# The second attention of a two-layer backbone: 18 filling steps set first, the others spread evenly and tied to the scores, bias tables requested at a group's middle, maxima two tiles later, eight raw weight buffers

## The chip, the core and the metric

The kernel runs on one core of a Trainium2 chip. Five engines work there side by side and meet at semaphores: PE (matrix products), DVE (vector), ACT (activation), POOL (a second, general vector engine) and SP, which here only issues transfers. Each engine takes its instructions in the order in which the built program lists them. An instruction that waits holds up everything behind it on the same engine. Transfers are issued by SP (a few by ACT) and carried out by 16 DMA engines that all queues share.

The metric is the device time of one launch in microseconds (us), the median of several runs. Beside it stands one profiled execution with its own time; all waits and durations below are from that one.

## What is computed

Two layers work on 1024 latent tokens and 256 context tokens of width 1024. Layer 0 is two kinds of grouped attention; layer 1, the odd one, joins a convolution branch (C) with a two-dimensional neighbourhood attention (D). The change is in layer 1, and there in D and in the product that follows it:

```python
cv, cgl, cg, dq, dk, dv, dg = split_cols(h_lat @ w_in, ODD_WIDTHS)
oc = conformer_conv(cv, cgl, cg, dw_w, dw_b, ln_g, ln_b)
def d_row(args):                       # one row of the 16x64 grid, all 8 heads
    r, qr = args
    rs = jnp.clip(r - kh // 2, 0, rows - kh)
    kr = lax.dynamic_slice_in_dim(k_grid, rs, kh, axis=1)   # 8 rows of keys
    ...
    bias = rpb[:, dr_idx][:, :, dc_idx] + col_mask[None, None]
    kk = jnp.concatenate([c_dk, kr], axis=1)                # 256 context keys first
    vv = jnp.concatenate([c_dv, vr], axis=1)
    return gqa_attend(qr, kk, vv, bias).reshape(bsz, GRID_W, D_W)   # softmax attention
od = lax.map(d_row, (jnp.arange(rows), q_rows))
y_lat = jnp.concatenate([oc, od * jax.nn.silu(dg)], axis=-1) @ w_out
x_lat = x_lat + g_l[:, None, :] * y_lat
return rms_norm(x_lat, final_g)
```

Everything is f32. The kernel splits each factor of a large product into a high and a low part and adds three matmuls, so that each such product counts three times.

## The kernel before, in words

**Groups and tiles.** The attention of layer 1 is cut into 16 groups: 8 heads (`hd`) times two column halves of the grid (`hf`). A group has 512 queries and seven score tiles: the context keys 0 to 127 (512 queries wide), five tiles of 128 grid keys (256, 352, 512, 320 and 224 queries wide) and the context keys 128 to 255 (512). A score tile `st` is two matmuls, L465 (`KAt` with `QH`) and L469 (`KBt` with `QL`). For the five grid tiles DVE adds the bias table `bs` (L474) and ACT takes the exponential (L475); for the context tiles ACT does it alone (L477). ACT casts the result to the high part `ph` (L296), POOL or DVE forms the low part `pl` (L299), and three matmuls L409 to L411 add it into the group's `ov`. There are two `st` banks. Each score tile's `ov` products are written in the code three tiles after it (`LOOK1`).

**Maxima.** Before a group's first score, its row maxima must be known. `maxes` makes six `mx` tiles on PE (L1342, L1350) from `QH` and the group's keys `KAt`; DVE reduces them (L1344, and L1351 together with the mask table `bm`); a transposition `trn` and L388 put them into `QL`. This preparation is done two groups ahead: at the start of group g the code asks for the queries of group g+2 (L1301 to L1303) and starts the maxima `LEAD` tiles later, four here.

**What a group's start requests.** `start` asks SP for the next group's bias table `bs` (832 KB, two buffers), at every other group for the next head's keys `KAt` (L361, two transfers of 384 KB, two buffers), and for this group's values `Vt`. Keys and queries go into buffers that the last score tile of the group before still reads, so they can be issued only after it. ACT copies the new keys' upper half into `KBt` (L555). In the group's middle `gate` asks for the gate values `gt` (L1320).

**Filling work.** The attention's own chain is long, so other matmuls are woven in: `d_proj(2)` and `d_proj(3)` (projections `p1` of the last four heads; 31 steps each of up to three dk, nine matmuls), `out1_part` (the output product `po1`: 32 steps with six matmuls, then 8), and `ends` (30 steps). `weave` runs `WV[i]` steps of the attention, two to a tile, and spreads a part's filling steps among them. The weights of a filling part come by `load_w` in pieces of 128 rows: SP loads a raw piece `wr` (L329, three buffers), ACT casts it to `wh` (L296), and POOL or DVE forms `wl` (L299).

**What sets the order.** The code is traced in program order; each instruction gets a priority from its place, and `later(FL[1])`, with -98, moves filling steps ahead. A list scheduler then simulates time and fixes each engine's queue: it takes, by priority, what its model of the chip holds to be ready, so an instruction written later can stand earlier. `issue_after` adds only an order between two instructions of one engine. With a lag of 0 for the first two parts, 6 and 12 for the others, a filling step is held behind the score that many tiles back, or not held at all.

The lines that the steps below touch are `d_proj` and `proj1` (L318 to L320 by way of `mm3`), `attn_gen`, `weave`, `gate`, `start`, `load_w`, and the calls at the end.

## Time and profile before

| | us |
|---|---|
| median of 3 runs (1557.06 to 1565.91) | 1563.07 |
| the profiled execution's own time | 1555.72 |
| its span, first to last instruction | 1553.9 |
| PE busy | 1449.1 |
| DVE, ACT, POOL busy | 1123.3, 759.8, 833.5 |

The profiled execution is 7.35 us shorter than the median and lies below all three runs but within half a percent of the median. A page of the profile gives busy times, which for PE are upper bounds since matmuls overlap; the windows view cuts the span into stretches and gives each engine's busy time, the granted PE clock (1.00 is full) and the share of the 16 DMA engines that was busy. The view of waits adds up, for each pair of line and releaser, how long the engine sat idle. In the names, `st<-QH,KAt` is written from right to left: `st` is made of `QH` and `KAt`. The second attention begins at 1212.7 us with the first maxima; its last score tile ends at 1516.9 us, and the program ends at 1553.9 us.

### The profile page before, as it was taken

What the parts mean: (1) busy time and instruction counts of PE and PEld (TensorE: products, weight loads), DVE (VectorE), ACT (ScalarE), POOL (GpSimd) and SP (SyncE); (2) the same over time, 40 slices, a digit from 0 to 9 for tenths busy, and PEclk for the clock granted to TensorE, in tenths of its full rate; (3) what the DMA queues carried; (4) which work ended last, traced back from release to release, by engine and by line L of the source; (5) the groups of instructions that cost most, each with busy time, mean ns of one, the idle gap of its engine ahead of it and who ended that gap; (6) DMA issues with size and microseconds to landing.
All of it is one profiled execution on the core that took longest, in us unless ns stands there. A gap on an engine that the chain in (4) does not pass through costs nothing.

```text
span 1553.9 us, 22052 instructions
## 1 busy us (share of the span) xinstructions
PE 1449.1 (93%) x6984; PEld 1172.3 (75%) x6984; DVE 1123.3 (72%) x2172; ACT 759.8 (49%) x1545; POOL 833.5 (54%) x762
## 2 busy tenths in 40 slices
PE   6989989999999989899999889999999999799995
PEld 1878868887789678678887668888787787687784
DVE  4998898689858666654577677999755457586776
ACT  2721354445454755565455555443434455545563
POOL 1561464555555676675455666664542443545574
PEclk9999999999999999999999999999999999899996
DMA  9548245423441124631111121213456888788623
GB/s 339 194 146 270 79 125 174 147 64 121 151 129 44 54 89 143 207 115 56 42 45 35 68 95 57 80 63 123 158 178 222 272 225 263 221 264 240 192 92 109
DMA packets 185614, 221.01 MB, mean 142 GB/s; under 512 B 17421, under 2 KB 139481, under 8 KB 185497
## 3 DMA queue, kind: packets, MB, share of 16 engines
q1 hardware_dynamic: 178832, 208.03, 43.1%
q10 hardware_dynamic: 6664, 11.57, 2.3%
q8 instruction: 55, 0.90, 0.2%
q14 instruction: 63, 0.51, 0.1%
HBM read 159.51 MB, written 60.03 MB: 141 GB/s over the span
## 4 chain that ended last, share of the span: by engine, by line
PE 67%; DVE 12%; DMA 11%; issue 3%; POOL 3%; ACT 2%; SPq 2%; DVEq 0%; ACTq 0%; POOLq 0%
PE p L320 6%; PE p L318 6%; PE p L319 6%; PE ov L409 4%; PE ov L410 4%; PE ov L411 4%; PE st L465 4%; PE po L318 4%; PE st L469 4%; PE po L319 4%; PE po L320 4%; PE pq L320 2%; PE pq L319 2%; PE pq L318 2%; DMA mw<-in_mod_w_dram 2%
## 5 line engine op out<-in xcount | busy, mean ns | idle before, releaser
L299 POOL TENSOR_TENSOR pl<-pf,ph 128x512 fp32r<-128x512 f32 (+4 forms) x321 | 399.9, 1258 | 270.7 <-ACT ph L296 218.9
L299 POOL TENSOR_TENSOR wl<-wr,wh 128x256 fp32r<-128x256 f32 (+2 forms) x256 | 197.7, 788 | 227.9 <-ACT wh L296 203.3
L477 ACT ACTIVATE pf<-st 128x512 f32<-128x512 f32 x284 | 166.2, 596 | 161.7 <-PE st L469 106.3
L296 ACT CAST ph<-pf 128x512 fp32r<-128x512 f32 (+4 forms) x364 | 209.2, 588 | 25.5 <-PE ov L410 17.6
L296 ACT CAST wh<-wr 128x256 fp32r<-128x256 f32 (+2 forms) x264 | 103.2, 404 | 172.2 <-DMA wr<-in_od_d_dram 39.3
L318 PE MATMUL p<-hh,wh 128*128 128x512 f32 x448 | 177.7, 399 | 3.7 <-DVE spk L299 1.4
L319 PE MATMUL p<-hl,wh 128*128 128x512 f32 x448 | 177.9, 398 | 0.2 <-POOL hl L299 0.2
L320 PE MATMUL p<-hh,wl 128*128 128x512 f32 x448 | 175.2, 399 | 0.1
L465 PE MATMUL st<-QH,KAt 128*128 128x512 f32 (+4 forms) x364 | 144.0, 397 | 19.8 <-ACT pf L477 16.5
L409 PE MATMUL ov<-ph,Vt 128*128 128x512 f32 (+4 forms) x364 | 143.6, 394 | 8.8 <-DVE y L631 6.4
L411 PE MATMUL ov<-pl,Vt 128*128 128x512 f32 (+4 forms) x364 | 143.7, 395 | 3.9 <-POOL pl L299 3.8
L410 PE MATMUL ov<-ph,Vt 128*64 128x512 f32 (+4 forms) x364 | 140.8, 387 | 0.0
L469 PE MATMUL st<-QL,KBt 68*128 68x512 f32 (+4 forms) x364 | 138.2, 388 | 0.8 <-DVE QL L388 0.7
L1116 DVE SCALAR_TENSOR_TENSOR cps<-U,taps,cps 128x512 f32<-128x512 f32 x184 | 124.3, 747 | 0.0
L589 DVE TENSOR_REDUCE mp<-mx 128x1 f32<-128x512 f32 x128 | 85.5, 682 | 33.5 <-PE mx L588 32.7
L219 DVE SCALAR_TENSOR_TENSOR macc<-mw,csil,macc 128x512 f32<-128x512 f32 x107 | 97.5, 929 | 14.0 <-DMA mw<-in_mod_w_dram 13.2
L318 PEld LDWEIGHTS p<-hh,wh 128*128 128x128 f32 x448 | 84.6, 189 | 24.5 <-DVE spk L299 1.6
L465 PEld LDWEIGHTS st<-QH,KAt 128*128 128x128 f32 x364 | 69.8, 192 | 42.5 <-ACT pf L477 25.3
L319 PEld LDWEIGHTS p<-hl,wh 128*128 128x128 f32 x448 | 84.6, 189 | 20.4 <-POOL hl L299 0.6
L320 PEld LDWEIGHTS p<-hh,wl 128*128 128x128 f32 x448 | 84.6, 189 | 20.3 <-POOL wl L299 1.0
L411 PEld LDWEIGHTS ov<-pl,Vt 128*128 128x128 f32 x364 | 71.1, 195 | 28.1 <-POOL pl L299 7.6
L409 PEld LDWEIGHTS ov<-ph,Vt 128*128 128x128 f32 x364 | 71.5, 196 | 24.3 <-issue 7.0
(277 smaller groups left out, 3518.4 us busy)
## 6 DMA issues: line engine op xcount, KB each, us to landing
mw<-in_mod_w_dram SPq DMA_DIRECT2D x34, 512.0 KB, 5.6
bs<-in_d_bs_dram SPq DMA_DIRECT2D x16, 832.0 KB, 7.3
Q<-qs SPq DMA_DIRECT2D x40, 256.0 KB, 2.7
QH<-Q SPq DMA_DIRECT2D x80, 128.0 KB, 2.7
bm<-in_d_bm_dram SPq DMA_DIRECT2D x16, 540.0 KB, 6.1
wr<-in_od_d_dram SPq DMA_DIRECT2D x64, 128.0 KB, 2.6
mw<-in_mod_w_dram SPq DMA_DIRECT2D x28, 256.0 KB, 3.1
wr<-in_ev_qkv_dram SPq DMA_DIRECT2D x32, 192.0 KB, 3.8
```

The source lines that it names most:

```text
L296: SC.copy(hi, src)
L299: (GP if leng == "g" else VE).tensor_tensor(lo, src, hi.bitcast(F32), op=ALU.subtract)
L318: PE.matmul(o, lh, rh, start=first, stop=False)
L319: PE.matmul(o, lh, rl, start=False, stop=False)
L320: done[0] = PE.matmul(o, ll, rh, start=False, stop=last)
L409: PE.matmul(o, V[:, 64:192], ph[:, :n], start=(t == 0), stop=False)
L410: PE.matmul(g.ov[0:64, q0 : q0 + n], V[:, 0:64], ph[:, :n], start=False, stop=False)
L411: pvs.append(PE.matmul(o, V[:, 64:192], pl[:, :n], start=False, stop=(last and g.sink is None)))
L465: sts.append(PE.matmul(st[:, :n], KA[:, cs], g.QH[:, q0 : q0 + n], start=True, stop=False))
L469: PE.matmul(st[:, :n], KB[0:68, cs], g.QL[0:68, q0 : q0 + n], start=False, stop=True)
L477: SC.activation(pf[:, :n], st[:, :n], AF.Exp, scale=1.0 if g.bias else SCALE)
L1116: VE.scalar_tensor_tensor(pc, uc, w, pc, op0=ALU.mult, op1=ALU.add)
```

## The change

No instruction's work changes; the two programs have the same score, value, weight and table transfers. What changes is the following.

- **18 steps first.** `PRE = 18` steps of `d_proj(2)` are written ahead of the attention's first step.
- **The rest even.** The remaining 44 steps of `d_proj(2)` and `d_proj(3)`, chained, are spread over the first 146 attention steps (before: 31 over 73, then 31 over 53). `out1_part` with 32 steps is spread over 57 (before 77); the last two parts keep 24 and 12.
- **Bound to the scores.** `TIE = 2`: a score tile's first matmul is put, in PE's queue, behind the last product of the filling step two steps back (`past[-2]`; `prods` is the list in which `mm3` leaves its last matmul). `LAG` becomes 4, 4 and 12: a filling step stands behind the score four tiles back in the first two parts.
- **Tables at the middle.** The request for the next group's `bs` moves from `start` to `gate`; only the first group's own table stays in `start`.
- **Later maxima.** `LEAD` for layer 1 goes from 4 to 6 tiles.
- **Eight raw buffers.** `WPR`, the raw weight buffers of `load_w` in layer 1, goes from 3 to 8.

```diff
-LEAD = (3, 4)
+LEAD = (3, 6)
...
-WPR = 3
+WPR = 8
...
-LAG = (0, 0, 6, 12)
-WV = (73, 53, 77, 24, 12)
+LAG = (4, 4, 12)
+PRE = 18
+WV = (146, 57, 24, 12)
...
+TIE = 2
...
-    done = [None]
+    done = prods = [None]
...
-            sts.append(PE.matmul(st[:, :n], KA[:, cs], g.QH[:, q0 : q0 + n], start=True, stop=False))
+            with ExitStack() as cx:
+                if tied[0] is not None:
+                    cx.enter_context(tc.issue_after(tied[0].ins))
+                sts.append(PE.matmul(st[:, :n], KA[:, cs], g.QH[:, q0 : q0 + n], start=True, stop=False))
...
-    def weave(main, nmain, fill, nfill, last=True, all_fill=True, lag=0):
+    def weave(main, nmain, fill, nfill, last=True, all_fill=True, lag=0, tie=0):
 
         done = 0
+        past = []
         for k in range(nmain):
+            tied[0] = past[-tie] if tie and len(past) >= tie else None
             next(main, None)
+            tied[0] = None
             while done * nmain < (k + 1) * nfill:
...
                     next(fill, None)
+                past.append(prods[0])
                 done += 1
...
             def gate():
                 g.gt = half("gt1")
                 SY.dma_start(g.gt[ds], GD[i][ds, hf])
+                for g2 in groups1[gi + 1 : gi + 2]:
+                    g2.load_bs()
 
             def start():
-                for g2 in groups1[gi + 1 if gi else 0 : gi + 2]:
-                    g2.load_bs()
+                if not gi:
+                    g.load_bs()
...
-        weave(main, WV[0], d_proj(2), 31, False, True, LAG[0])
-        weave(main, WV[1], d_proj(3), 31, False, True, LAG[1])
+        d2 = d_proj(2)
+        for _ in range(PRE):
+            with later(FL[1]):
+                next(d2)
+        weave(main, WV[0], chain(d2, d_proj(3)), 62 - PRE, False, True, LAG[0], TIE)
         run(out1_alloc())
-        weave(main, WV[2], out1_part(range(4)), 32, False, True, LAG[2])
+        weave(main, WV[1], out1_part(range(4)), 32, False, True, LAG[1], TIE)
...
-        weave(main, WV[3], out1_part((4, 5, 6), (1,)), 8, False, True, LAG[3])
+        weave(main, WV[2], out1_part((4, 5, 6), (1,)), 8, False, True, LAG[2])
```

What the scheduler makes of it stands in three places. The line numbers of the changed program are a few higher (L465 becomes L471, L469 L475, L318 L321, L1342 L1354).

The first is PE's queue in the seventh group (the fourth head's first half). Each `st` is a score tile's two matmuls, `ov` the value products, `p` a filling projection. Before:

```order
L465 MATMUL st_14018<-QH_13421,KAt_12382 128x352
L469 MATMUL st_14018<-QL_13422,KBt_12383 128x352
L411 MATMUL ov_13802<-pl_13889,Vt_12386 128x512
L465 MATMUL st_14052<-QH_13421,KAt_12382 128x512
L469 MATMUL st_14052<-QL_13422,KBt_12383 128x512
L465 MATMUL st_14087<-QH_13421,KAt_12382 128x320
L469 MATMUL st_14087<-QL_13422,KBt_12383 128x320
L409 MATMUL ov_14073<-ph_13924,Vt_12385 128x512
L410 MATMUL ov_14073<-ph_13924,Vt_12385 64x512
L411 MATMUL ov_14073<-pl_13925,Vt_12385 128x512
```

and now, from the same score tile on:

```order
L471 MATMUL st_14034<-QH_13551,KAt_12382 128x352
L321 MATMUL p_3498_14076<-hh_9770,wh_13897 128x512
L322 MATMUL p_3498_14076<-hl_9771,wh_13897 128x512
L323 MATMUL p_3498_14076<-hh_9770,wl_13898 128x512
L321 MATMUL p_3498_14076<-hh_9770,wh_13903 128x512
L322 MATMUL p_3498_14076<-hl_9771,wh_13903 128x512
L323 MATMUL p_3498_14076<-hh_9770,wl_13904 128x512
L321 MATMUL p_3498_14076<-hh_9770,wh_13909 128x512
L322 MATMUL p_3498_14076<-hl_9771,wh_13909 128x512
L323 MATMUL p_3498_14076<-hh_9770,wl_13910 128x512
L475 MATMUL st_14034<-QL_13552,KBt_12383 128x352
L414 MATMUL ov_13843<-pl_13946,Vt_12386 128x512
```

Where three score tiles stood almost side by side, a whole filling step now stands between a tile's two halves.

The second is SP's queue at the start of the third group, where `bs` is a bias table, `KAt` the next head's keys, `QH` and `QL` queries. Before:

```order
L1314 DMA bs_12989<-in_d_bs_dram 128x1664
L361 DMA KAt_12379<-KD_7314 64x1536 x2
L1301 DMA QH_12995<-QD_7310 64x512
L1302 DMA QH_12995<-QD_7310 64x512
L1303 DMA QL_12996<-QD_7310 64x512
L1305 DMA bm_13209<-in_d_bm_dram 128x1080
```

and now:

```order
L364 DMA KAt_12379<-KD_7314 64x1536 x2
L1311 DMA QH_13133<-QD_7310 64x512
L1312 DMA QH_13133<-QD_7310 64x512
L1313 DMA QL_13134<-QD_7310 64x512
L1324 DMA bs_13279<-in_d_bs_dram 128x1664
```

The table moved from ahead of keys and queries to behind them. At the starts of the ninth, eleventh and thirteenth groups it stood between the two key transfers or just behind them, and it too is now behind the queries; at the fifth and seventh it still stands ahead of the keys.

The third is PE's queue in the ninth group, up to the first maxima `mx` of the eleventh, which read keys and queries requested at the ninth group's start. Before, with `po` a filling product:

```order
L465 MATMUL st_14567<-QH_13914,KAt_12379 128x512
L469 MATMUL st_14567<-QL_13915,KBt_12380 128x512
L318 MATMUL po_3665_14717<-oc_14459,wh_14500 128x512
L319 MATMUL po_3665_14717<-oc_14459,wh_14500 128x512
L320 MATMUL po_3665_14717<-oc_14459,wl_14501 128x512
L318 MATMUL po_3665_14717<-oc_14459,wh_14506 128x512
L319 MATMUL po_3665_14717<-oc_14459,wh_14506 128x512
L320 MATMUL po_3665_14717<-oc_14459,wl_14507 128x512
L1342 MATMUL mx_3634_14603<-KAt_12382,QH_14427 128x256 x2
```

and now:

```order
L412 MATMUL ov_14273<-ph_14253,Vt_12386 128x512
L413 MATMUL ov_14273<-ph_14253,Vt_12386 64x512
L414 MATMUL ov_14273<-pl_14254,Vt_12386 128x512
L471 MATMUL st_14356<-QH_13969,KAt_12379 128x512
L475 MATMUL st_14356<-QL_13970,KBt_12380 128x512
L390 MATMUL trn_14390<-ident,nmt_14378 4x128
L412 MATMUL ov_14273<-ph_14280,Vt_12386 128x320
L413 MATMUL ov_14273<-ph_14280,Vt_12386 64x320
L1354 MATMUL mx_3617_14522<-KAt_12382,QH_14349 128x256 x2
```

Before, the maxima stood behind the group's fourth score tile; now they stand behind its first.

3 lines of the change are left out of this document (2 added, 1 removed).

## The prediction

> **What bounds the kernel now.** I read the page first, then windows over the second attention, then PE's waits there, then single stretches of the timeline, and the landing times of the transfers behind them.
>
> ```profile
> span 1553.9 us, 22052 instructions
> PE 1449.1 (93%) x6984; PEld 1172.3 (75%) x6984; DVE 1123.3 (72%) x2172; ACT 759.8 (49%) x1545; POOL 833.5 (54%) x762
> PE 67%; DVE 12%; DMA 11%; issue 3%; POOL 3%; ACT 2%; SPq 2%; DVEq 0%; ACTq 0%; POOLq 0%
> ```
>
> PE carries two thirds of the chain that ended last. The change removes no PE work, so it can win only what PE loses in the stretch it touches: idle time and granted clock.
>
> ```profile
> 1212.00:1402.00 190.00, 176.06 (x872) 142.98 (x873) 127.26 (x310) 98.81 (x210) 79.42 (x85) 0.96 0.84 247
> 1402.00:1516.00 114.00, 109.07 (x518) 88.28 (x517) 80.30 (x177) 67.80 (x144) 70.82 (x76) 0.99 0.61 177
> 1340.00:1350.00 10.00, 5.69 (x18) 3.69 (x18) 4.52 (x10) 3.28 (x7) 4.11 (x5) 0.76 1.05 248
> 1350.00:1360.00 10.00, 7.18 (x27) 6.30 (x28) 4.15 (x10) 6.30 (x13) 4.73 (x5) 0.56 0.72 180
> 1440.00:1450.00 10.00, 6.88 (x29) 5.03 (x28) 7.42 (x16) 4.28 (x9) 2.41 (x3) 0.88 1.01 247
> 1450.00:1460.00 10.00, 10.00 (x51) 8.40 (x50) 4.12 (x12) 7.35 (x16) 8.94 (x9) 0.95 0.58 180
> ```
>
> The columns are the stretch, its length, busy time of PE, weight load, DVE, ACT and POOL, then the granted clock, the share of the DMA engines and GB/s. The second attention runs from 1212 to 1516. PE is idle there for 13.9 + 4.9 = 18.8 us, and loses 0.04 x 190 + 0.01 x 114 = 8.7 us to the clock: 27.5 us is the whole prize, 1.8%. Half lies in one place: from 1340 to 1360 PE is idle for 7.1 us and loses 2.4 + 4.4 = 6.8 us of clock.
>
> ```profile
> PE mx L1342 <- DMA KAt<-KD: 4.7, 2, 2.8
> PE mx L1342 <- DMA gt<-GD: 3.2, 1, 3.2
> PE st L465 <- DVE pf L474: 2.8, 3, 1.8
> PE st L465 <- ACT pf L477: 2.1, 2, 1.8
> PE p L318 <- DVE r L421: 1.1, 1, 1.1
> PE trv L1226 <- ACT vc L1206: 0.8, 1, 0.8
> PE p L318 <- ACT wh L296: 0.2, 1, 0.2
> ...
> 1342.88 0.43 PE L465 MATMUL st<-QH,KAt 128*128 128x352 f32 x1 [1.79 <-ACT pf L477]
> 1345.98 0.64 PE L465 MATMUL st<-QH,KAt 128*128 128x320 f32 x1 [1.82 <-DVE pf L474]
> 1352.82 0.77 PE L1342 MATMUL mx<-KAt,QH 128*128 128x256 f32 x2 [3.22 <-DMA gt<-GD]
> ```
>
> Two kinds of wait make the prize: maxima that wait for keys or queries (4.7 + 3.2 = 7.9 us; the row that names `gt` is the same wait, for the queries queued with it), and scores that wait for their bank (4.9 us). The bank waits belong to the seventh group, from 1338 on, where the filling projections had run out and PE had only scores and values to do.
>
> **The change part by part.** *18 steps first.* Ahead of the first maxima both orders hold the same five projections of `d_proj(2)`; from the start of the third of them, 14.2 us of PE work now stands ahead of these maxima, 13.5 before. PE work is counted here and below in columns, at 0.234 us from start to start for 512, as in three rows of the chain:
>
> ```profile
> 1218.07 0.23 PE p L318
> 1218.30 0.24 PE p L319
> 1218.54 0.23 PE p L320
> ```
>
> So 0.7 us more cover for the first maxima: -0.7. They wait for the first keys, which need the buffers of the convolution's last stage; that does not move.
>
> *Even and tied.* In columns at that price, the third to ninth groups were 17, 18, 15, 18, 6, 10 and 16 us of PE work long and are now 16, 17, 13, 14, 12, 17 and 13. The two short groups get filling, and the products with `pl` now stand at least 3.8 us of work behind their scores (before, ten stood within 4 us, seven of them in the sixth and seventh groups). Of the 4.9 us of bank waits I leave 1: -4. The two small waits in the rows (1.1 and 0.8) belong to switches of weights for which raw pieces will now be there: -2. The clock loss follows the long waits: 6.8 us in the one stretch and 1.2 + 0.5 us after 1440 become, for the one long wait of the next paragraph and some shorter ones, about 3: -5.5.
>
> *Maxima, keys and queries.* This speaks against the change. Keys and queries can be requested only when the last score of the previous group is done, and PE stops at the first maxima until they land. What counts is the PE work between those two points. For the second to eleventh groups it was 8.1, 10.1, 9.1, 6.5, 7.7, 4.8, 5.8, 11.1, 6.8 and 10.8 us; it is now 5.6, 6.9, 2.8, 8.2, 2.6, 8.8, 7.7, 3.1, 6.7 and 6.8, and in the thirteenth 5.4 for 8.8. `LEAD` is later in the code, but the scores now wait for filling steps, so the scheduler pulls maxima in. Against it stands what the landings cost with and without a table ahead:
>
> ```profile
> KAt<-KD SPq DMA_DIRECT2D x2, 384.0 KB, 5.1
> KAt<-KD SPq DMA_DIRECT2D x2, 384.0 KB, 9.2
> KAt<-KD SPq DMA_DIRECT2D x2, 384.0 KB, 10.3
> QH<-QD SPq DMA_DIRECT2D x2, 128.0 KB, 2.8
> QH<-QD SPq DMA_DIRECT2D x2, 128.0 KB, 3.9
> QH<-QD SPq DMA_DIRECT2D x2, 128.0 KB, 8.2
> ...
> 1259.07 1.09 SPq L361 DMA_DIRECT2D KAt<-KD  x2
> 1260.85 0.59 SPq L1302 DMA_DIRECT2D QH<-QD  x1
> ```
>
> These are issues of the transfers view at 1368 (keys first), 1258 and 1338 (keys behind `bs`), 1316 and 1385 (queries with no table ahead) and 1241 (behind `bs` and a weight piece); the last two rows are SP's timeline at 1259. Where keys and queries go first I take 5.1 and the 1.8 us by which the second query piece is issued after the keys, 6.9 us, nearer to 5.1 than to 9.2 since no table is ahead; for queries alone 3.9; for the second group, whose queries still follow a table, 8.2. The waits, landing less work, are then 2.6 (second group), 0, 1.1, 0, 1.3, 0, 0, 3.8 (ninth), 0, 0.1 and 1.5 (thirteenth): 10.4 us for 7.9. The same count with 9.2 and 10.3 behind tables gives for before 2.7 + 5.5 + 0.4 + 0.1, or 8.7, so the method holds: +2.5. Its ends are 2 us of waits (5.1 and 2.8 everywhere) and 31 us (9.2 and 8.2 everywhere).
>
> The Trainium skill would price a landing lower: "DMA: Bandwidth & Descriptors", section "Anatomy of one DMA", gives about 2.0 us plus bytes over 436 GB/s, an estimate of 4.4 us for two key and two query pieces. By it almost no maxima would wait and the sum would come to that of the first rival. The trace disagrees: two key pieces alone took 5.1 us here at a DMA share of 0.84.
>
> *ACT's copy of the keys.* L555 stands in ACT's queue and waits for the same keys.
>
> ```profile
> ACT KBt L555 <- DMA KAt<-KD: 19.6, 7, 4.6
> ACT wh L296 <- DMA wr<-in_od_d_dram: 11.9, 7, 4.2
> SPq L329 <- POOL wl L299: 50.7, 37, 5.7
> ```
>
> Behind it stand casts and exponentials. In the ninth group it has moved ahead of the casts of the eighth's last two grid tiles, whose `ov` products PE meets before the maxima; in the third, seventh and eleventh it has moved up by two to four rows. The keys' first half releases it, sooner than the maxima, so most of this lies inside the waits above; the copy itself (1.5 us) and the rest of ACT's backlog do not: +1.5, between 0 and 6.
>
> *Tables at the middle.* The order shows the table only a few rows later, behind the queries, because its buffer has long been free when the middle comes. It then has a whole group, at least 11 us of PE work, against 7.3 us to land:
>
> ```profile
> bs<-in_d_bs_dram SPq DMA_DIRECT2D x16, 832.0 KB, 7.3
> ```
>
> Nothing, between 0 and +3; the gain is in the landings above. The Trainium skill's rule is to issue a DMA early and wait for it late ("DMA: Bandwidth & Descriptors", section "Rules for kernel authors"), which speaks against the move; by these rows it costs nothing here.
>
> *Eight raw buffers.* They remove ACT's waits for raw pieces and SP's waits in front of them (the two rows above). PE waited 0.2 us for a weight in all, so the cover is the filling already in PE's queue: 0, between -3 and +2, since up to eight pieces of 128 KB now go out in one burst ahead of other requests. The layer's earlier stages lose little PE time: 0.
>
> *Denser maxima.* The eight `mx` tiles from the first group's last to the third group's first now stand with three score passes between them.
>
> ```profile
> L1351 DVE CUSTOM_DVE_ANT_0 mx<-mx,bm 128x440 f32<-128x440 f32 (+1 forms) x64 | 35.0, 559 | 19.8 <-PE mx L1350 19.8
> L1344 DVE TENSOR_REDUCE mp<-mx 128x2 f32<-128x512 f32 x32 | 21.9, 684 | 18.3 <-PE mx L1342 18.1
> ```
>
> DVE needs 8 x 0.6, some 5 us, where PE has about 2.5 us of work: up to +3, of which part is hidden behind earlier landings. I take +1.
>
> The sum: -0.7 - 4 - 2 - 5.5 + 2.5 + 1.5 + 1 = -7.2 us. The end after the last score is the same but for two products that now stand ahead of a broadcast. Against the profiled 1555.7 us that is 1548.5; the median of the runs stood 7.4 us above that execution, so for a median it is 1556 us.
>
> **The rivals.** *Landings are quick.* If the keys come in 5.1 and the queries in 2.8 us because no table and no stalled weight request stands ahead of them, waits fall to 2 instead of 10.4 us and the clock loss by another 1: -17, or 1546 for a median. For it speaks SP's 50.7 us behind raw buffers, which go; against it, that those waits did not stand ahead of keys or queries where I looked.
>
> *The transfers become the bound (the other side).* The 190 us of the first stretch hold ten groups and 0.84 x 190 = 160 us of all DMA engines' work; the first ten groups are now 147 us of PE work, with fewer filling steps and their traffic beside them. If the share passes about 0.95 in the first groups, keys land as behind a table, 9.2 us, and queries in 8.2: 31 us of waits. The stalls relieve the queue, so I count 24, 14 more than in the forecast, and 6 us more of clock: +13, or 1576.
>
> *The change does not do what it says.* The scheduler's clock is not the chip's: weights of a filling step that are late now hold the scores too, by the tie, and what the even spread wins at the seventh group is lost at the three switches of weights. The waits would move and the sum stay: 1563.
>
> The Trainium skill's "TensorE: Matmul & The Clock Gate" (section "HAM oscillation") says that idle gaps over about 3.4 us halve the clock. The rows agree roughly: 0.56 granted after the wait that ended at 1352.8. It would touch one of my waits, the ninth group's 3.8 us.
>
> **How the numbers follow.** My forecast has 0.40, quick landings 0.26, the transfers' bound 0.24, no effect 0.10. The forecast's own range is -14 to 0. The range over all reaches from quick landings, with a little of the unknown costs and of the spread of the runs (1557 to 1566 before), 1539, to the transfers' bound, 1577. The bound for a difference is half a percent, 7.8 us, about what a measurement of this kernel can tell. Faster by more: not quite half of the forecast's chance and nearly all of the quick landings, 0.43. Slower: nearly all of the transfers' bound and a little of the rest, 0.25. Within: 0.32.
>
> **What the profile will show.** Right: no stretch like 1340 to 1360; no `st` wait for `pf` above 1 us; waits of `mx` or `ov` in the ninth and thirteenth groups for keys, queries or the casts behind ACT's copy. Wrong on the fast side: `mx` waits under 4 us in sum and a clock of 0.99 throughout. Wrong on the slow side: a DMA share over 0.95 from 1212 to 1300 with waits of several us in the second to sixth groups, or scores that wait for filling weights.

## The result

The changed kernel takes 1566.7 us (median, 1562.72 to 1577.39), the kernel before 1560.85 us: a ratio of 1.0039, with a 95% interval from 1.0024 to 1.0055. It is slower by 5.9 us where 7 us less were forecast; the difference lies within the half percent of the "no change" case.

The page of the changed kernel, and two windows that answer to those from 1212 to 1516 before (the first maxima now stand at 1218.8, the last group's first score at 1503.4):

```profile
span 1566.7 us, 22105 instructions
PE 69%; DVE 14%; DMA 8%; issue 4%; POOL 3%; ACT 2%; SPq 1%; ACTq 0%; DVEq 0%; POOLq 0%
...
1215.00:1405.00 190.00, 171.72 (x812) 136.46 (x811) 121.64 (x301) 97.99 (x203) 78.68 (x84) 0.93 0.80 238
1405.00:1521.00 116.00, 114.75 (x555) 93.79 (x554) 84.06 (x180) 66.97 (x144) 72.79 (x78) 1.00 0.63 185
```

DMA's share of the chain fell from 11 to 8%. The second half is now nearly perfect: 1.3 us idle and a clock of 1.00. The first 190 us are worse than before, and it is the clock that makes them so: 0.07 x 190 = 13.3 us are lost to it (7.6 before). Of their 18.3 us of idle time (13.9 before), 2.4 us come from where the window begins: it opens 3.8 us ahead of the first maxima, inside the wait for the first keys, and the window of before 0.7 us ahead of them. Counted alike, from the first maxima to the last group's first score, PE is idle for 16.5 us where it was 18.1. PE's waits there:

```profile
PE mx L1354 <- DMA QH<-QD: 4.7, 4, 2.2
PE st L471 <- DVE pf L480: 3.6, 6, 1.2
PE mx L1354 <- DMA KAt<-KD: 3.1, 1, 3.1
PE ov L412 <- DVE y L1379: 2.2, 4, 1.3
PE ov L412 <- ACT ph L299: 1.7, 1, 1.7
PE mx L1362 <- DVE mp L1363: 1.3, 2, 0.9
PE mx L1362 <- DVE mp L1356: 0.8, 3, 0.4
PE st L471 <- ACT pf L483: 0.8, 1, 0.8
```

The long waits (3.2 and 2.8 us for keys and queries, a pair of 1.8 for banks) are gone, and the longest that is left is that for the first keys. The sum is little smaller, because waits of 1 to 2 us have come up in other places.

Below, "loss" is the time from one product's start to another's, less the columns between them at 0.2335 us for 512 columns. It holds idle time, clock loss and whatever else a product takes beyond its columns, such as pauses too short for the profile to count as idle. By groups, each from its first score to the next group's (the first from the first maxima), in us of PE work / loss:

| group | before | changed | three buffers (e1) | loose bond (t5) |
|---|---|---|---|---|
| 1 | 26.4 / 3.0 | 19.7 / 7.9 | 20.0 / 4.5 | 19.8 / 5.3 |
| 2 | 18.9 / 0.5 | 12.2 / 7.5 | 12.5 / 4.8 | 14.3 / 0.9 |
| 3 | 17.6 / 1.2 | 16.8 / 1.3 | 16.9 / 4.9 | 20.2 / 1.6 |
| 4 | 15.5 / 0.1 | 14.6 / 0.1 | 14.6 / 0.7 | 15.3 / 0.1 |
| 5 | 21.9 / 5.4 | 13.0 / 7.1 | 13.0 / 6.5 | 19.5 / 0.1 |
| 6 | 11.4 / 3.7 | 14.1 / 2.1 | 14.0 / 0.6 | 19.3 / 0.5 |
| 7 | 7.0 / 12.7 | 15.0 / 3.4 | 14.9 / 4.1 | 15.5 / 5.1 |
| 8 | 12.8 / 1.3 | 16.7 / 2.2 | 16.9 / 2.0 | 15.1 / 3.2 |
| 9 | 15.9 / 0.4 | 10.7 / 7.3 | 10.7 / 7.5 | 14.1 / 1.8 |
| 10 to 15 | 9.8 lost | 4.3 lost | 7.2 lost | 17.7 lost |
| sum of losses | 38.0 | 43.1 | 42.8 | 36.2 |

The 5.1 us between the two sums are clock (10.2 us before, 13.7 now) and the remainder (9.6 before, 13.0 now); idle time fell by 1.6. The parts overlap a little, since a wait that falls into half speed counts in both, and no run separates what the remainder is made of.

Losses repeat from one execution to another where the order is the same: in e5 and e6, which have the changed order up to the last score, the sum was 45.2 both times and the first, second, fifth and ninth groups lost 6 to 10 us again; in t4, with the order of before, it was 37.9.

Of the 12.8 us between the two profiled spans 3.4 arise ahead of the first `trv` (1104.5 and 1107.9 us); that point lay between 1103.7 and 1114.8 in all profiled executions, whatever the kernel (1103.7 in one with the changed order, e5), so it isn't counted to the change here. Then 2.7 us come before the first maxima (2.1 of it work that moved there), 2.8 from the first maxima to the last group (2.3 us less work, 5.1 more loss), and 4.0 from the last group's first score to the end (63.3 for 59.3).

### The profile page after: what moved, and what is told of

Its sections match the earlier page's. It is cut to its first block, busy times and chain, and to the rows that moved or that the text cites. A ratio compares the mean times of both kernels' runs of the same rounds, so it can differ in the third digit from the quotient of the medians.

```text
span 1566.7 us, 22105 instructions
## 1 busy us (share of the span) xinstructions
PE 1460.2 (93%) x6984; PEld 1180.9 (75%) x6984; DVE 1130.2 (72%) x2172; ACT 758.7 (48%) x1545; POOL 834.5 (53%) x762
## 4 chain that ended last, share of the span: by engine, by line
PE 69%; DVE 14%; DMA 8%; issue 4%; POOL 3%; ACT 2%; SPq 1%; ACTq 0%; DVEq 0%; POOLq 0%
PE p L323 6%; PE p L322 6%; PE p L321 6%; PE ov L412 4%; PE po L321 4%; PE po L323 4%; PE po L322 4%; PE ov L414 4%; PE ov L413 4%; PE st L471 4%; PE st L475 4%; PE pq L323 2%; PE pq L321 2%; PE pq L322 2%; PE pg L321 2%
## 5 line engine op out<-in xcount | busy, mean ns | idle before, releaser
L299 ACT CAST ph<-pf 128x512 fp32r<-128x512 f32 (+4 forms) x364 | 209.0, 589 | 18.9 <-PE ov L413 11.2
L321 PE MATMUL p<-hh,wh 128*128 128x512 f32 x448 | 177.6, 398 | 2.0 <-DVE spv L302 1.0
L471 PE MATMUL st<-QH,KAt 128*128 128x512 f32 (+4 forms) x364 | 144.5, 398 | 17.2 <-ACT pf L483 13.3
L412 PE MATMUL ov<-ph,Vt 128*128 128x512 f32 (+4 forms) x364 | 143.9, 395 | 11.6 <-DVE y L641 6.1
L299 ACT CAST wh<-wr 128x256 fp32r<-128x256 f32 (+2 forms) x264 | 100.0, 404 | 111.2 <-DMA wr<-in_ev_qkv_dram 35.7
L475 PE MATMUL st<-QL,KBt 68*128 68x512 f32 (+4 forms) x364 | 138.3, 388 | 0.9 <-DVE QL L391 0.5
L222 DVE SCALAR_TENSOR_TENSOR macc<-mw,csil,macc 128x512 f32<-128x512 f32 x107 | 97.4, 928 | 12.6 <-DMA mw<-in_mod_w_dram 11.8
L321 PEld LDWEIGHTS p<-hh,wh 128*128 128x128 f32 x448 | 85.1, 190 | 21.7 <-issue 1.6
L471 PEld LDWEIGHTS st<-QH,KAt 128*128 128x128 f32 x364 | 70.0, 193 | 40.6 <-ACT pf L483 21.0
```

The lines of the kernel that those rows point to most:

```text
L299: SC.copy(hi, src)
L321: PE.matmul(o, lh, rh, start=first, stop=False)
L412: PE.matmul(o, V[:, 64:192], ph[:, :n], start=(t == 0), stop=False)
L471: sts.append(PE.matmul(st[:, :n], KA[:, cs], g.QH[:, q0 : q0 + n], start=True, stop=False))
L475: PE.matmul(st[:, :n], KB[0:68, cs], g.QL[0:68, q0 : q0 + n], start=False, stop=True)
```

## The experiments

Ratios are to the kernel before in the same sitting, with 95% intervals.

**Each part by itself.** e1 is the changed kernel with three raw buffers. e2 has the spread alone, e3 the eight buffers alone, e4 the tables alone.

```diff
-LEAD = (3, 6)
+LEAD = (3, 4)
-WPR = 8
+WPR = 3
...
             def gate():
...
-                for g2 in groups1[gi + 1 : gi + 2]:
-                    g2.load_bs()
...
             def start():
-                if not gi:
-                    g.load_bs()
+                for g2 in groups1[gi + 1 if gi else 0 : gi + 2]:
+                    g2.load_bs()
```

That is e2's edit of the changed kernel; e1 has the line of `WPR` alone. e3 sets `WPR = 8` in the kernel before, e4 puts the two pieces of `gate` and `start` there the other way round.

> The changed kernel with three raw weight buffers again (everything else of the change stays). Theory A: the loss comes from the eight buffers. With them the scheduler packs the seven maxima tiles of the second group and the first of the third within 1.6 us of PE work, DVE cannot follow, PE pauses in small pieces and its clock is halved for 6 us; with three buffers the same tiles lie over some 12 us of PE work. Then this kernel is about 5 us faster than the changed one, 1559 to 1563, no different from before, and the stretch from the first maxima to the third group keeps a clock of 1.00. Theory B: the even spread bound to the scores costs the time itself (scores wait at their bank and for filling steps). Then it stays at 1565 to 1568.

> The kernel before with the 18 steps first and the even, bound filling alone: three raw buffers, the bias tables asked for at a group's start, the earlier lead of the maxima. Theory A: 1554 to 1561, at or below the kernel before, since the stall of 13 us at the seventh group is gone and nothing packs the maxima. Theory B: 1565 to 1570, as the changed kernel. Theory C, the tables at the middle are what costs (their landing meets the keys): faster than the run with three buffers by 3 us or more.

> The kernel before with eight raw weight buffers and nothing else. Theory A: slower than before by 3 to 8 us, 1564 to 1569: the filling steps run ahead, four groups in the middle are left with 6 to 12 us of PE work and wait for keys and for score banks. Theory B: no difference, 1559 to 1563, since PE waited 0.2 us for weights before.

> The kernel before with the bias tables asked for in the middle of a group, and nothing else. If keys and queries land sooner without a table ahead of them, 1556 to 1560. If the order that the scheduler then makes (less PE work between the request of keys and their maxima, 2.5 to 6 us where 6 to 11 stood) eats that, 1561 to 1566. Theory C (tables at the middle cost): 1564 or more.

Measured: e1 1567.15 us, 1.0034 (1.0019 to 1.0049). e2 1568.89 us, 1.0053 (1.0032 to 1.0074). e3 1580.83 us, 1.012 (1.0098 to 1.0142). e4 1564.18 us, 1.0017 (0.9998 to 1.0036). So theory A falls: without the eight buffers the time is the same, and the spread alone costs what the whole change costs, as theory B has it. C falls too, since e2 is not faster than e1. e3 lies above the ranges of both A and B. The reason that A gave is visible all the same. With eight buffers the first two groups lose 15.4 us, with three 9.3 (the first group 7.9 and 4.5); but with three the third group and those after the ninth lose 6.5 us more. In the changed kernel the packed maxima look like this (clock windows from 1229.18):

```profile
1229.18:1232.59 3.41, 2.48 (x11) 1.21 (x9) 3.04 (x9) 0.00 (x0) 0.00 (x0) 1.00 1.06 376
1232.59:1236.00 3.41, 3.30 (x9) 2.67 (x10) 2.74 (x9) 1.94 (x4) 1.17 (x1) 0.50 0.76 232
1236.00:1239.41 3.41, 3.41 (x10) 2.72 (x9) 0.24 (x1) 0.00 (x0) 0.80 (x2) 0.50 0.37 142
```

DVE is busy for 3.04 of 3.41 us, PE pauses in pieces, and then runs at half speed for 6.8 us. The waits of e2 and then of e3 (sum, times, longest):

```profile
PE mx L1352 <- DMA QH<-QD: 11.2, 6, 5.7
PE mx L1352 <- DMA xs<-X: 2.7, 1, 2.7
PE mx L1352 <- DMA KAt<-KD: 2.5, 2, 2.0
...
PE st L471 <- DVE pf L480: 1.9, 4, 0.8
...
PE st L471 <- ACT pf L483: 0.4, 2, 0.2
```

```profile
PE mx L1342 <- DMA QH<-QD: 13.5, 6, 4.3
PE st L465 <- DVE pf L474: 2.9, 5, 0.9
```

In e2 the bank waits fell from 4.9 to 2.3 us, the way that was forecast for the change (to 1), but those for keys and queries rose from 9.2 (4.7, 3.2 and 1.3 that name `KAt`, `gt` and `QH`) to 16.4. (Like the row with `gt`, the one that names `xs` is a wait of first maxima for queries: they were requested at 1413.6 us, a piece landed at 1423.4, and the wait ended at 1423.9.) In e3 the scheduler pulls filling ahead (30 us of work in the first group); the fifth to seventh groups are left with 7 to 10 us and lose 24.

**Without the bond.** e8 sets `TIE` to 0 and the first two lags to 0 and keeps the rest of the change.

> The changed kernel without the bond: filling steps wait for no score and scores for no filling step; 18 steps first, even counts, eight buffers, lead and tables stay. The scheduler then puts filling early (28 us in the first group) and has 6 to 10 us groups from the tenth to the fourteenth. Theory B (the bond to the scores costs): 1558 to 1563. Rival (without the bond filling runs out, as in the kernel before with eight buffers, which took 1581): 1568 to 1580.

Measured: 1572.15 us, 1.0097 (1.0078 to 1.0117). Filling went early, the first nine groups lost little after the first (6.0, then 0.0 to 4.0), and the tenth to fourteenth lost 34 us. The time lies in the rival's range: with eight buffers the kernel is slower still without the bond. What the bond itself costs within the change this run doesn't tell, since it has another order.

**The end.** Nothing in the end is touched by the change, yet its order moved. POOL from the second piece's last sum on, the changed kernel and then the kernel before (start, length, instruction):

```profile
1549.65 0.75 POOL L1480 TENSOR_TENSOR sq<-sq,sq 128x256 f32<-128x256 f32 x1 [1.91 <-ACT sq L1476]
1550.91 0.89 POOL L241 TENSOR_TENSOR nr<-rbv,mhalf 128x2 f32<-128x2 f32 x1 [0.51 <-DVE rbv L257]
1551.78 0.72 POOL L1480 TENSOR_TENSOR sq<-sq,sq 128x256 f32<-128x256 f32 x1
1554.67 2.77 POOL L1496 TENSOR_TENSOR x<-x,bcs 128x256 f32<-128x256 f32 x4 [2.17 <-ACT bcs L1491]
1557.39 0.71 POOL L241 TENSOR_TENSOR nr<-rbv,mhalf 128x2 f32<-128x2 f32 x1
```

```profile
1538.72 0.72 POOL L1468 TENSOR_TENSOR sq<-sq,sq 128x256 f32<-128x256 f32 x1 [2.63 <-ACT sq L1464]
1539.88 0.72 POOL L1468 TENSOR_TENSOR sq<-sq,sq 128x256 f32<-128x256 f32 x1 [0.44 <-ACT sq L1464]
1540.56 0.89 POOL L238 TENSOR_TENSOR nr<-rbv,mhalf 128x2 f32<-128x2 f32 x1
1543.35 0.69 POOL L238 TENSOR_TENSOR nr<-rbv,mhalf 128x2 f32<-128x2 f32 x1 [1.90 <-DVE rbv L254]
1544.62 2.77 POOL L1484 TENSOR_TENSOR x<-x,bcs 128x256 f32<-128x256 f32 x4 [0.58 <-ACT bcs L1479]
```

Before, both sums stand ahead of both rsqrt (`nr`), which follow each other by 2.8 us. Now the last sum stands behind the first rsqrt, and the last rsqrt behind four products: 6.5 us apart. e5 gives the last sum to DVE; e6 also holds PE's sums `trs` of the second piece behind the last output tile; t4 does e5's edit to the kernel before.

```diff
-SQP = ((2, 3, 4, 5, 6), (), (4, 6))
+SQP = ((2, 3, 4, 5, 6), (), (4,))
```

e6 has this and:

```diff
-EVS = "e1 c1 e2 f1 c2 f2".split()
+EVS = "e1 e2 c1 f1 c2 f2".split()
+                elif ev == "c1":
+                    with tc.issue_after(prods[0].ins):
+                        bcs[k] = yield from rstd_steps(dpool, sums[k], ENDS[k][2], BCT[k])
```

> The changed kernel, with one instruction moved: the sum of squares of the seventh output tile in the last piece goes to DVE instead of POOL. Everything up to the last score stands in the same order. In the changed kernel POOL has this sum behind the rsqrt of the second piece and the last rsqrt behind four products of 0.7 us; before, sum and rsqrt stood ahead of them. Theory D (the end has become longer): the end after the first product of the last output stage shrinks from 25 to about 20.5 us, and the kernel runs in 1561 to 1564, 4 to 5 us less than the changed one. Theory B (the loss lies in the groups of the second attention): 1565 to 1568, since the end is within what the runs vary.

> The same as the run with the last sum, and PE's sums of the second piece held behind the last output tile's products, as in the kernel before; so the end has the order of before, and all the rest that of the changed kernel. Theory D: the end takes 18 us, 1558 to 1561, no longer slower than before; the whole 5.9 us of the change lay in the end. Theory B: 1564 or more.

> The kernel before with the last sum of squares on DVE instead of POOL; all else in the order of before. Theory D: the end of before has no swap to mend, so 1559 to 1563, no difference; its stretch of the second attention shows the losses of the kernel before again, some 45 us from the first maxima to the last output stage, with 12 us in the seventh group.

Measured: e5 1563.15 us, 1.0033 (1.0018 to 1.0048); e6 1562.62 us, 1.0032 (1.0013 to 1.0052); t4 1564.29 us, 1.0017 (0.9995 to 1.0039). In the profiles the rsqrt are 2.8 us apart again in e5, and the end takes 60.8 us in e5 and 61.1 in e6 where the changed kernel took 63.3. So undoing the swap is worth some 2.5 us in these profiles, of which the edit alone may bring a part: in t4, where there is no swap to undo, it shortened the end from 59.3 to 58.1. In the ratio, with its interval of 0.15% to either side, 2.5 us can't be told from nothing, and e6's second edit brings nothing. Besides, 1.7 us of work moved into the end. e5's time lies within theory D's range, but the kernel before was faster in that sitting too, and the ratio is still 1.0033; e6 misses its range. Theory D, that the whole loss lies in the end, falls. Of the 20 profiles only those of the changed kernel and of e3 have the swapped order; e1 and e2 don't, and are as slow.

**The clock.** e7 puts products of identity by identity ahead of the fourth and seventh groups' first maxima, in the bank that these overwrite.

```diff
+ALIVE = {3: (262, 8), 6: (284, 10)}
...
                         mx = bank("mx", nm("mx1"))
+                        if b and gi in ALIVE:
+                            with tc.issue_after(sts[ALIVE[gi][0]].ins):
+                                for _ in range(ALIVE[gi][1]):
+                                    PE.matmul(mx[:, 0:P], ident, ident, start=True, stop=True)
```

> The changed kernel with added work for PE: 8 products of identity by identity (128 columns) into the bank of the fourth group's first maxima, right ahead of them, and 10 at the seventh group's; the real products then overwrite them. PE waits there for queries and keys (1.6 and 2.2 us), and the clock was halved for 6.8 us behind each. Theory E (the clock is granted by windows of 3.4 us, and one in which PE was busy less than about half is followed by half speed): both stay at 1.00, which is worth 3.4 us each, and the added work lies in the waits: 1560 to 1563, if the 4 us are hidden. Rival (the clock falls by something else, or the waits are not there in this run): 1566 to 1570, up to 4 us slower.

Measured: 1563.34 us, 1.0031 (1.0011 to 1.0051). The windows around the seventh group's first maxima, first of the changed kernel, then of e7:

```profile
1307.69:1311.10 3.41, 1.20 (x6) 0.91 (x6) 1.97 (x5) 3.41 (x9) 1.98 (x3) 1.00 1.16 238
1311.10:1314.52 3.42, 3.16 (x10) 2.30 (x10) 3.31 (x10) 0.22 (x1) 1.56 (x2) 0.50 0.88 263
1314.52:1317.93 3.41, 3.41 (x12) 2.85 (x12) 1.97 (x6) 1.09 (x3) 0.87 (x1) 0.50 0.23 51
```

```profile
1307.45:1310.87 3.42, 3.42 (x27) 3.00 (x27) 2.51 (x7) 2.24 (x4) 0.00 (x0) 1.00 1.03 226
1310.87:1314.28 3.41, 3.26 (x21) 2.55 (x20) 2.79 (x7) 2.31 (x6) 3.08 (x4) 1.00 1.05 253
```

The time lies just above theory E's range and below that of its rival. At both places the clock stayed at 1.00: the second group's loss fell from 7.5 to 4.3 us, the fifth's from 7.1 to 2.9. (A group's loss here holds the maxima that are made in it for the group two later, and in e7 the added products.) That is the 7 us that theory E asked for, locally. But the added work moved the scheduler's later choices, and the tenth and eleventh groups lost 4.3 and 4.4 us where the changed kernel lost 0.8 and 1.2; the time is 0.8 thousandths better than the changed kernel's, which the intervals can't tell from nothing.

**Maxima held.** e9 is the changed kernel with every product of the maxima issued behind the score that the code has ahead of it; e10 adds `WPR = 3`; e11 does the same edit, with a lead of six, to the kernel before; e12 to e2.

```diff
-                            PE.matmul(mx[:, k * 256 : (k + 1) * 256], QH[:, bb[k] * P : (bb[k] + 1) * P], KA[:, 0:256],
-                                      start=True, stop=True)
+                            with tc.issue_after(sts[-1].ins):
+                                PE.matmul(mx[:, k * 256 : (k + 1) * 256], QH[:, bb[k] * P : (bb[k] + 1) * P], KA[:, 0:256],
+                                          start=True, stop=True)
...
-                    PE.matmul(mx[:, :n], QH[:, b * P : (b + 1) * P], KA[:, o : o + n], start=True, stop=True)
+                    with tc.issue_after(sts[-1].ins):
+                        PE.matmul(mx[:, :n], QH[:, b * P : (b + 1) * P], KA[:, o : o + n], start=True, stop=True)
```

> The changed kernel with one edit: every product of the maxima is held behind the score that stands ahead of it in the code, so that the scheduler cannot pull it up and LEAD takes effect. Between the last score that frees keys and queries and their first maxima stand now 11 to 18 us of PE work in the second to eleventh groups, 3 to 9 in the changed kernel; the last sum of the end is ahead of the rsqrt again. Theory F (landings of 5 to 10 us against too little work, and the half-speed windows behind the waits, are the price of the even spread): waits of maxima for keys and queries fall from 7.8 us to that for the first keys alone, and the losses at the fourth, seventh and ninth groups go: 1550 to 1556, faster than before by 3 to 9 us. Rival (the waits move to scores and values, DVE being late with maxima that now meet the softmax's work): 1560 to 1566.

> The run before with three raw buffers, so that the second group's maxima are spread over 12 us of PE work instead of 1.4. Theory F with the packed maxima as a cost of their own (some 5 us idle and half-speed clock from the first maxima to the third group in all three profiles of the changed order): 2 to 5 us faster than with eight, 1546 to 1553. If the packed maxima cost nothing by themselves: the same as with eight. If raw pieces are short with three: slower by 2 us or more.

> The kernel before with the same hold on the maxima and a lead of six, and nothing else: the filling is uneven as before. Its waits for keys and queries (7.9 us, three of the four half-speed stretches at or behind them) should go; its bank waits of the seventh and eighth groups stay, since the short groups stay short (9.5 to 12 us). Theory F: 1550 to 1556. If holding the maxima only moves the waits: 1559 to 1563.

> The run of the spread alone (which was slower than before by half a percent) with the maxima held and a lead of six: tables at a group's start, three raw buffers. Theory F: the 16 us of waits for keys and queries of that run go, with their half-speed windows, and it is 15 to 20 us faster than it was, 1546 to 1553. Where tables in the middle are worth something, the run with three buffers above is faster than this one; where the cover of 11 to 18 us holds even landings of 9 to 10 us behind a table, both are the same.

Measured: e9 1568.67 us, 1.0063 (1.004 to 1.0086); e10 1565.39 us, 1.0031 (1.0009 to 1.0052); e11 1574.48 us, 1.0095 (1.0066 to 1.0124); e12 1566.69 us, 1.0035 (1.0013 to 1.0056). Theory F falls, in all four; e9 and e11 lie above their rivals' ranges too, e11 by 11 us. e9's waits show where the time went:

```profile
PE st L471 <- DVE pf L480: 8.6, 11, 1.5
PE mx L1355 <- DMA KAt<-KD: 4.0, 1, 4.0
PE ov L412 <- ACT ph L299: 2.6, 1, 2.6
```

The waits for keys and queries did go, but for the first keys. In their place scores wait for their bank, 8.6 us for 3.6. The bias addition on DVE that frees the bank comes later, and maxima that now stand among the scores are a part of the reason: during those waits DVE worked 2.4 us on maxima (`mx`, `mp` and `nmt` in its timeline), 0.2 us in the changed kernel. The rest went to bias additions and to finishing groups, so the 5 us are not all traced to the maxima. e10 against e9 (three buffers against eight) is 3 thousandths better, though the intervals overlap; its first two groups lose 9.1 us for 14.7, most of the difference in the first, where the packed maxima stand.

**Shares of the filling.** t1 and t2 are e1 with the last sum on DVE and other shares; t3 holds t1's first maxima lightly, with a lead of four; t5 and t6 start from the kernel before.

t1 (t2 has 120 and 83), and the lines that t3 puts around the first tile of a group's maxima:

```diff
-WV = (146, 57, 24, 12)
+WV = (110, 93, 24, 12)
...
+HOLD = 2
...
+                                if b and gi > 1:
+                                    cx.enter_context(tc.issue_after(sts[-HOLD].ins))
```

t5, from the kernel before (t6 has 56, 63 and 84):

```diff
-LAG = (0, 0, 6, 12)
-WV = (73, 53, 77, 24, 12)
+LAG = (8, 8, 6, 12)
+WV = (50, 60, 93, 24, 12)
...
-        weave(main, WV[0], d_proj(2), 31, False, True, LAG[0])
+        d2 = d_proj(2)
+        for _ in range(10):
+            with later(FL[1]):
+                next(d2)
+        weave(main, WV[0], d2, 31 - 10, False, True, LAG[0])
```

> The run with three buffers (1.0034 of before), with the 44 remaining filling steps spread over the first 110 steps of the attention instead of 146, the first steps of the output projection over the next 93 instead of 57, and the last sum on DVE. The first ten groups then have 23, 19, 17, 16, 19, 16, 14, 13, 15 and 14 us of PE work where the changed kernel has 20, 12, 17, 15, 13, 14, 15, 17, 11 and 17. Theory G (a group with less than about 14 us of PE work pays the rest as idle time and half-speed clock, since DVE is busy 12 to 14 us in each and keys take 5 to 10 us after the last score): the groups that lost 7 us each (second, fifth, ninth) lose under 3, 1553 to 1560, not slower than before. Rival (the waits follow the landings wherever the filling stands): 1563 to 1567.

> The same with the 44 steps over the first 120 (the next over 83): 23, 15, 17, 16, 16, 14, 17, 13, 16 and 14 us of PE work in the first ten groups. Theory G: 1553 to 1560 as well, within 2 us of the run above. If the first groups alone matter: 1 to 3 us slower than the run above, since the second group has 15 us instead of 19.

> The first run of these with the first maxima of each group held behind the score two before, at a lead of four: 7 to 13 us of PE work between last score and maxima where that run has 5 to 10; the other maxima are free. If waits for keys and queries are what is left: 3 to 6 us faster than that run. If DVE is what is left (scores waiting for their bank while DVE does maxima): the same or slower.

> The kernel before with ten filling steps first, each further step held behind the score eight before, and shares of 50, 60 and 93 for the three stages of filling where it has 73, 53 and 77. PE work of the first ten groups: 20, 14, 20, 15, 20, 19, 16, 15, 14 and 13 us (before: 26, 19, 18, 16, 22, 11, 7, 13, 16, 14), with 10 to 13 us ahead of the maxima of most groups. Theory G with the cover for keys: the 12 us of the seventh group go and little comes in their place: 1549 to 1556. Rival (an even share only moves the waits, to DVE and to banks): 1560 to 1565.

> The same with shares of 56, 63 and 84: 18, 15, 17, 20, 16, 20, 15, 16, 17 and 14 us; but two of the ten steps fall behind the first maxima, so 11.7 us of PE work cover the first keys instead of 13.5. Theory G: 1549 to 1557, within 3 us of the run above. Rival: 1560 to 1565.

Measured: t1 1563.61 us, 1.0024 (1.0005 to 1.0044); t2 1561.83 us, 1.0014 (0.999 to 1.0039); t3 1564.15 us, 1.0023 (1.0003 to 1.0042); t5 1560.59 us, 1.0012 (0.9998 to 1.0027); t6 1562.44 us, 1.0018 (0.9999 to 1.0036). t1, t2, t5 and t6 lie above theory G's ranges, t1, t5 and t6 in those of the rivals, and t3 is no faster than t1. Theory G is right in its places: t1's second, fifth and ninth groups have 18.7, 18.5 and 14.8 us of work and lose 1.4, 1.3 and 2.4. It is wrong in the sum: t1 loses 2 to 5 us in each of the nine groups from the sixth to the fourteenth, and t5, with 14 us or more in the first nine, gives back 17.7 us from the tenth to the fifteenth. Loss in the middle (first maxima to the last group's first score), with the clock's part, and the length of the end, in us:

| | loss (clock) | end |
|---|---|---|
| before; t4 | 38.0 (10.2); 37.9 (10.2) | 59.3; 58.1 |
| changed; e5; e6 | 43.1 (13.7); 45.2 (13.7); 45.2 (12.6) | 63.3; 60.8; 61.1 |
| e1; e2; e3; e4 | 42.8 (11.9); 47.7 (11.9); 54.1 (17.1); 40.5 (11.9) | 60.4; 60.4; 62.2; 58.2 |
| e7; e8 | 41.2 (8.5); 48.1 (18.2) | 60.6; 61.9 |
| e9; e10; e11; e12 | 47.4 (20.0); 40.6 (6.8); 55.2 (18.8); 45.0 (13.2) | 59.1; 60.1; 59.6; 60.0 |
| t1; t2; t3 | 39.9 (3.4); 42.5 (8.5); 36.9 (6.8) | 61.0; 59.7; 59.5 |
| t5; t6 | 36.2 (10.2); 34.4 (6.8) | 60.3; 60.0 |

No variant beat the kernel before. The lowest losses in the middle, 34.4 and 36.2, go with a time that can't be told from that of the kernel before.

## Why the prediction was wrong

The forecast was -7.2 us, and +5.9 was measured. The mechanism that it saw, the seventh group's stall, did go: 12.7 us of loss became 3.4, and the thirteenth group's 5.3 became 0.4. What failed is the sum of what came in its place, the clock above all. The terms for idle time add up to -1.7 us (all but the clock's), and idle time up to the last group's first score did fall, by 1.6, while the wait for the first keys grew by 1.1. That this comes near is luck, since the terms were off one by one and cancelled.

- **Clock loss, -5.5: the step that failed most.** It left about 3 us, for one long wait and "some shorter ones". From the first maxima to the last group's first score 13.7 us were lost to the clock, 10.2 before: +3.5. Five stretches of half speed replaced three: after the wait for the first keys (3.1 us), after the packed maxima (longest wait 0.4 us, but PE busy for 2.48 of 3.41 us), and after pauses of 1.6, 2.2 and 1.7 us. Waits that short had been counted for next to nothing. The rows of before already spoke against that. The forecast took the 0.56 after 1350 as the price of the 3.2 us wait that ended at 1352.8, but the clock had been halved since 1345.15, behind two bank waits of 1.8 us each:

```profile
1341.74:1345.15 3.41, 1.29 (x5) 0.81 (x5) 1.47 (x5) 2.25 (x5) 2.32 (x3) 1.00 1.09 261
1345.15:1348.56 3.41, 2.52 (x6) 1.76 (x7) 2.77 (x6) 0.50 (x1) 0.36 (x1) 0.50 0.96 192
```

- **Bank waits, -4:** 4.4 us were left of 4.9, so -0.5. In e2 they did fall, to 2.3.
- **Small waits at weight switches, -2:** they went (0.2 us is left for `spv`), but `ov` for `y`, 2.2 us that no term had, came up: nothing in place of -2. The longest of these waits is the seventh group's. DVE stood idle until the last `ov` product of the group before came, and then needed until 1345.74 to finish that group; PE waited for it:

```profile
1341.36 0.45 DVE L422 STREAM_TRANSPOSE r<-ov 64x256 f32<-64x256 f32 x1 [2.64 <-PE ov L414]
1344.90 0.84 DVE L1379 TENSOR_TENSOR y<-ov,rb 64x256 f32<-64x256 f32 x2
1345.89 0.47 PE L412 MATMUL ov<-ph,Vt 128*128 128x512 f32 x1 [1.27 <-DVE y L1379]
```

- **Keys and queries, +2.5:** it set 10.4 us against 7.9, but the 7.9 hold the first keys' 1.9, which the 10.4 leave out, and leave out the 1.3 of the row that names `QH`. Without the first keys it was 7.3 us before and is 4.7 now: -2.6. The price of keys with no table ahead, 5.1 us, was near (4.3 to 6.9 from the third group on); the places were not. The fourth, sixth and thirteenth groups have no wait for them over 0.3 us, the ninth 0.5 us for its 3.8, since PE already waited for casts. The fifth, for which 0 stood, waited 2.2: its table still stood ahead of the keys, as the order under "The change" has it, and they took 8.2 and 9.0 us.
- **ACT's copy, +1.5:** the 1.7 us of `ov` for `ph` stand in the ninth group, as said, and the copy `KBt` stands ahead of the cast. Right:

```profile
1372.87 1.47 ACT L565 CAST KBt<-KAt 64x1536 fp32r<-64x1536 f32 x1 [2.16 <-DMA KAt<-KD]
1374.25 0.73 ACT L299 CAST ph<-pf 128x320 fp32r<-128x320 f32 x2
```

- **Tables, 0 up to +3:** e4 measured +2.7 alone, with an interval that includes no change at all. Within the bounds.
- **Eight buffers, 0 (-3 to +2):** within the change e1 finds nothing for them in the time, as the term had it. In the kernel before they cost 1.2%, 19 us: that PE waited only 0.2 us for weights said nothing on what the scheduler does once weights are early. SP's waits behind raw buffers, which were to go, fell from 50.7 to 30.0 us.
- **Denser maxima, +1 (up to 3):** the idle time was near, but not the price. The first group loses 7.9 us, with three buffers (e1) 4.5; the two windows of half speed behind the packed maxima are worth 3.4 of that. PE's waits for `mp` in the first two groups are only 0.4 and 0.2 us. The order showed this packing; the term left out the clock behind it.
- **18 steps first, -0.7:** the first maxima waited 3.1 us for keys in place of 1.9 (4.7 less 2.8 in the row before). The 2.1 us of work that moved ahead of them covered nothing, since the keys came later too: 6.3 us from request to landing, 4.2 before. This goes with eight buffers under the changed order. In the changed kernel and e5 to e9, eight weight pieces are requested in the 12 us ahead of the first keys and these land in 5.3 to 6.6 us; in the 14 other profiles, e3 among them, it is five pieces and 4.2 to 4.9 us. That is the burst that the term for eight buffers named.
- **The end, "the same":** wrong by 4 us, some 2.5 of it the order on POOL. The term rested on PE's order alone.

Of the rivals the one that "does not do what it says" (1563) is nearest: the waits moved and the sum stayed. Its mechanism isn't the one found, though: no score waited for a filling weight. The transfers did not become the bound: the share was 0.80 in the 190 us where 0.84 stood before, and 0.77 from 1212 to 1300. Of the signs on the slow side none showed. Of the right ones the stretch like 1340 to 1360 is gone and the ninth group waits for casts, but `st` waited for `pf` up to 1.2 us, and the thirteenth group hardly waits.

What stays open: from the first `trv` on, the profiled executions put 8.5 to 11.6 us between the changed order (458.8, 457.9 and 459.8 us) and that of before (449.4 and 448.2), more than the 5.9 us of the medians. The two of before's order lay 5 and 8 us under their medians, those of the changed order 0 to 4 above, and no run tells why. Where the filling should stand is open as well: e7 won 7.4 us at two places by holding the clock and lost the gain in later groups, so that the clock is the cause of the whole difference is argued from the traces, not shown by a run. What the remainder of the loss is (13.0 us, 9.6 before) and why the last `ov` product ahead of the seventh group comes late was not tried.

## What to carry to other kernels

Filling moved into a stall is taken from somewhere: before spreading it evenly, write down for each group the PE work that stays against what the other engines and the next transfer need, and look for the groups that fall short. Where a scheduler fixes the order, a change of buffers or leads can move instructions in stages that it doesn't name; compare the order of every engine up to the end of the program. A wait can't be priced by its length alone if the clock is granted by how busy PE was.

## What the runs showed of the hardware

All changes of PE's granted clock in these traces lie on a grid of 3.413 us, and the stretches of half speed before the program's end are one to four such steps long. Cutting the stretch from 1150 to 1500 us of the 20 profiled executions along each one's grid, a window at full speed in which PE was busy for less than half was followed by half speed in 73 of 75 cases; between 0.5 and 0.7 in 21 of 80, between 0.7 and 0.9 in 6 of 203, above 0.9 in none of 1539. (Each count moves by a few with how exactly the grid is laid.) From half speed, none of 27 windows under 0.8 led back. So a wait of 1.6 or 1.7 us, as in the changed kernel, can cost another 1.7 or 3.4 us (one or two windows), by where it falls in the grid. Between 0.5 and 0.7 no rule was found; in the kernel before, of two windows with 62% the first was followed by full speed and the second by half:

```profile
1300.77:1304.19 3.42, 2.14 (x13) 1.57 (x13) 1.46 (x4) 3.09 (x6) 0.00 (x0) 1.00 1.08 231
1304.19:1307.60 3.41, 2.11 (x10) 1.18 (x8) 3.32 (x10) 1.21 (x3) 0.93 (x1) 1.00 1.05 377
1307.60:1311.02 3.42, 3.38 (x8) 2.73 (x9) 3.42 (x9) 2.94 (x6) 0.00 (x0) 0.50 1.05 382
```

The Trainium skill's "TensorE: Matmul & The Clock Gate", section "What's actually happening", describes a free-running window of 3413 ns, with which the grid agrees. The Trainium skill's rule in section "HAM oscillation" of the same page is to avoid idle gaps over about 3.4 us. The trace differs, and the measurement decides here: the window ahead of 1311.10 had 1.20 of 3.41 us busy, its longest gap, 2.2 us, began 0.4 us ahead of it, and it was followed by half speed.
